# Strassen partial sums in a decoder trunk: banks emptied by ScalarE, the sum finished later on VectorE

## The chip, the core and the metric

The kernel is one program on one core of a Trainium2 chip. The metric is the device time of one execution in microseconds (us). A core has five engines that run side by side, each with a queue of its own: TensorE (PE in the profile, with its weight loads as PEld), VectorE (DVE), ScalarE (ACT), GpSimd (POOL) and SyncE (SP); the last two issue most of the DMA transfers here. A matmul adds its result into a bank of PSUM, the buffer that only TensorE, VectorE and ScalarE reach; a bank holds 128 x 512 float32.

## The reference

The reference is a trunk of two decoder layers on 512 tokens of width 1024. Each layer normalises, makes one wide projection, runs three attention-like branches, merges them by gates, projects and adds the residual. Then comes the part that the change touches, a squared-ReLU MLP:

```python
h = rmsnorm(x, norm_mlp_g[l])
x = x + jnp.square(jax.nn.relu(h @ w_up[l])) @ w_down[l]
```

with `w_up` of 1024 x 4096 and `w_down` of 4096 x 1024. A final RMSNorm closes the trunk. The result must agree with float32.

## The kernel before

Every operand of a product is split into a high and a low part of a matmul type that keeps fewer bits (`hi` by a cast on ScalarE, `lo` by a subtraction on VectorE, `split_to` and `Weights.split`), and each product is three matmuls: hi x hi, lo x hi, hi x lo. Weights come in by DMA, are split two units ahead (`W.pump`) into four pairs of buffers `whi`/`wlo`, and each unit is used by 12 or 24 matmuls.

The MLP runs over four groups `g` of 1024 hidden channels in each of the two layers. In groups 0 to 2 the down projection (512 x 1024 times 1024 x 1024) is done by Strassen's scheme in `strassen`: seven products of half-size blocks in place of eight. First eight calls of `tile_T` make the hidden activations, tile by tile (`put_h` squares them on ScalarE into the blocks `H[t, i, q]`, where tile m fills i = m // 4, q = m % 4 // 2). Sums and differences of these blocks are the left operands: `ready_early` after tile 3 makes those of P1 and P7, `ready_sums` after tile 7 makes S1 and S2 in two halves q (lines 1552 and 1553) and splits S2 for P6; P4, P5, P2 and P3 follow from `split_part` and `ready_s4`. The products run in the order P1, P7, P6, P4, P5, P2, P3, each as 24 matmuls (lines 1585 to 1587) in two units u of 12, into a pair of PSUM banks: P1, P6, P5 and P3 add up in the pair "B", P7 and P4 in "D", P2 in "A". A pair that goes on accumulating must be read out between two products: `add_to` (line 1598) reads both banks after P1 for the first output block, after P6 for the next, and so on. So it runs seven times a group, on two banks each time. An output block `acc[key]` that is not there yet is written by ScalarE (line 1605). One that is there is updated by one VectorE instruction that reads the bank, scales it and adds it (line 1607). In a layer's group 0 eight of the fourteen read-outs are first ones; groups 1 and 2 have none. After group 3's up projection has begun, `fold` transposes `acc` back and adds it to the residual.

The order is set in two steps. In the program, `defer(fn, delay)` puts evacuations and operand work in the queue `later`, which `run_later` serves as the dense products advance a clock of estimated nanoseconds; `need(name)` forces it. Then the compiler's scheduler lays the program out on the engines by a timeline of its own and may put instructions of one engine in another order than the program has them. On the chip each engine runs its own list in that fixed order, and semaphores hold an instruction back until its inputs and buffers are ready. Temporaries of 128 x 512 come from 42 slots (`get`, `put`).

Of the kernel before, what the change touches and what calls it, by code (L numbers as in the profile page):

```python
# [13 lines left out]
AF = mybir.ActivationFunctionType  # L14
ALU = mybir.AluOpType
# [33 lines left out]
class Weights:  # L49
# [33 lines left out]
    def block(self, kind, srcs):  # L83

        c = len(self.chunks)
        self.chunks.append((srcs, 4, 512))
        self.left.append(None)
        self.queues[kind].append(c)
        return c
# [138 lines left out]
def trunk_kernel(  # L228
# [15 lines left out]
    nc = tc.nc  # L244
# [12 lines left out]
    def get(dtype=F32):  # L257
        i = slots.popleft()
        t = sb.tile([P, 512], dtype, name=f"slot{i}", tag=f"slot{i}")
        owner[id(t)] = (i, t)  # L260
        return t

    def get2():
        return get(R), get(R)

    def put(*ts):
        for t in ts:
            slots.append(owner.pop(id(t))[0])
# [59 lines left out]
    clock = {"t": 0}  # L328
# [5 lines left out]
    def defer(fn, delay=0):  # L334
        later.append((clock["t"] + delay, fn))

    def run_later():
        while later and later[0][0] <= clock["t"]:
            later.popleft()[1]()

    def flush():
        while later:
            later.popleft()[1]()
# [53 lines left out]
    def drive(dense):  # L397
        for y in dense:
            if isinstance(y, tuple):
                if y[0] == "start":  # L400
                    live.append([y[1], clock["t"], y[2], None])
                elif y[0] == "finish":
                    finish()
                continue
            clock["t"] += y
            run_later()
            W.pump()
            advance()
# [172 lines left out]
    def split_to(hi, lo, src, g=None):  # L581

        if g is None:
            nc.scalar.copy(hi, src)
            nc.vector.tensor_sub(lo, src, hi.bitcast(F32))
        else:
            nc.scalar.activation(hi, src, AF.Copy, scale=g)
            nc.vector.scalar_tensor_tensor(lo, in0=src, scalar=g, in1=hi.bitcast(F32), op0=ALU.mult, op1=ALU.subtract)
# [42 lines left out]
    def tile_T(xs, evac):  # L631

        got, [(hi, lo)] = W.take()
        ps = dense_psum()
        nk = len(xs)
        yield from mm_T(ps, [hi[:, k] for k in range(nk)], [lo[:, k] for k in range(nk)], xs)
        W.done(got)
        evacuate(ps, lambda: evac(ps))
# [417 lines left out]
    def layer(l, box):  # L1056
# [381 lines left out]
        scale = {}  # L1438
# [14 lines left out]
        def put_up(m):  # L1453
            def go(ps):
                hi, lo = get2()
                h = get()
                nc.scalar.activation(h, ps, AF.Relu)
                nc.vector.tensor_mul(h, h, h)
                split_to(hi, lo, h)
                put(h)  # L1460
                hid[m] = (hi, lo)

            return go

        def put_down(m, final):
            def go(ps):
                t = get()
                nc.vector.tensor_mul(t, ps, rstd2_b)
                nc.vector.tensor_add(xm[m], xm[m], t)
                put(t)  # L1470
                if final:
                    new_x(m, G_MIX + (l + 1) * KD)
                    nc.gpsimd.dma_start(x_dram[l + 1][m], xm[m])
                    put(xm.pop(m))

            return go

        def put_last(m, c):
            def go(ps):
                q = get()  # L1480
                v = xm[m][:, c]
                nc.vector.tensor_mul(q[:, :256], ps[:, :256], rstd2_b[:, c])
                nc.vector.tensor_add(v, v, q[:, :256])
                nc.scalar.activation(q[:, :256], v, AF.Square)
                nc.scalar.activation(v, v, AF.Copy, scale=gain[:, G_FIN + m : G_FIN + m + 1])
                if m == KD - 1:
                    stats["t"] = q
                elif "s" not in stats:
                    stats["s"] = q
                else:  # L1490
                    nc.vector.tensor_add(stats["s"][:, :256], stats["s"][:, :256], q[:, :256])
                    put(q)

            return go

        def output(c):
            s, t = stats.pop("s"), stats.pop("t")
            r = to_rstd(token_sums([s, t], 2), D, 2)
            ps = rot(tt)
            spread_to(ps, r, 2)  # L1500
            for m in range(KD):
                nc.vector.tensor_mul(xm[m][:, c], xm[m][:, c], ps[:, :256])
                nc.sync.dma_start(out[m * P : (m + 1) * P, c], xm[m][:, c])
            put(s, t)


        acc = {}

        def strassen():

            H, parts = {}, {}
# [14 lines left out]

                return go

            def split_part(name, src, free=True):
                got = parts[name] = []  # L1530
                for q in range(2):
                    hi, lo = get2()
                    split_to(hi, lo, src[q])
                    got.append((hi, lo))
                if free:
                    put(*src)

            def block(t, i):
                return [H[t, i, q] for q in range(2)]
# [6 lines left out]
                    nc.vector.tensor_sub(s[q], H[0, 0, q], H[1, 0, q])  # L1546
                split_part("P7", s)

            def ready_sums():

                for q in range(2):
                    nc.vector.tensor_sub(H[1, 0, q], H[1, 1, q], H[1, 0, q])
                    nc.vector.scalar_tensor_tensor(
                        H[0, 0, q], in0=H[1, 0, q], scalar=-1.0, in1=H[0, 0, q], op0=ALU.mult, op1=ALU.subtract
                    )
                split_part("P6", block(0, 0), False)

            def ready_s4():

# [35 lines left out]
            def add_to(bank, i, j, sign):  # L1595


                def go():
                    for t in range(2):
                        ps = banks[bank][t]  # L1600
                        r = scale[sign][:, 2 * i + t : 2 * i + t + 1]
                        key = (2 * i + t, j)
                        if key not in acc:
                            acc[key] = get()
                            nc.scalar.activation(acc[key], ps, AF.Copy, scale=r)
                        else:
                            nc.vector.scalar_tensor_tensor(
                                acc[key], in0=ps, scalar=r, in1=acc[key], op0=ALU.mult, op1=ALU.add
                            )

                return go

# [6 lines left out]
            for m in range(KD):  # L1619
                yield from tile_T(X, put_h(m))  # L1620
                if m == 3:
                    defer(ready_early)
            defer(ready_sums)
            need("P1", parts)
            yield from product("P1", "B", True, False)
            defer(add_to("B", 0, 0, "+"))
# [23 lines left out]
            defer(give("B"))  # L1650

        def need(name, parts):
            while name not in parts:
                later.popleft()[1]()

        def fold(m):


            def go():
                ps = rot(tt)  # L1660
                for t in range(NT):
                    a = acc[t, m // 4][:, m % 4 * P : (m % 4 + 1) * P]
                    nc.tensor.transpose(ps[:, t * P : (t + 1) * P], a, ident)
                nc.vector.tensor_add(xm[m], xm[m], ps)
                if m % 4 == 3:
                    put(*(acc.pop((t, m // 4)) for t in range(NT)))

            return go

        for g in range(4):  # L1670
            if g < 3:
                if g == 2 and l < DEPTH - 1:
                    W.retired.extend(hold["pairs"])
                yield from strassen()
                continue
            for m in range(KD):
                defer(fold(m), 3000 + 4000 * m)
            if l < DEPTH - 1:
                W.retired.append(hold["wide"])
            for m in range(KD):  # L1680
                yield from tile_T(X, put_up(m))
            if (l, g) == (DEPTH - 1, 3):
                for hf in range(2):
                    c = slice(hf * 256, hf * 256 + 256)
                    for m in range(KD):
                        yield from tile_T(Later(hid, KD, c), put_last(m, c))
                    defer(lambda c=c: output(c))
                return
            for m in range(KD):
                yield from tile_T(Later(hid, KD), put_down(m, g == 3))  # L1690

            def free_h(hs):
                for hi, lo in hs:
                    put(hi, lo)

            hs = [hid.pop(k) for k in range(KD)]
            defer(lambda hs=hs: free_h(hs))
# [10 lines left out]
    def trunk():  # L1708
        for l in range(DEPTH):
            yield from layer(l, box)  # L1710
# [67 lines left out]
```

## Time and profile before

| | |
|---|---|
| median of 3 runs | 1824.52 us (1823.94 to 1825.95) |
| profiled execution | 1823.96 us, span 1822.2 us |
| PE busy | 1795.6 us (99%) |
| DVE busy | 1136.8 us (62%) |
| ACT busy | 805.5 us (44%) |
| POOL busy | 91.1 us (5%) |
| granted PE clock, mean | 0.997 |

The profiled execution's time is 1.76 us above its span; the span is what the profile resolves. PE is busy almost throughout, but its busy time counts overlapping matmuls, so how fast it goes is read from the spacing of matmul starts. Times in the rows below are microseconds from the start of the span.

### The profile page before, as it was taken

To read this page: it belongs to the slowest core of one execution; us is meant where nothing else is said; L and a number is where in the kernel's file an instruction comes from. 1 tells how busy PE (TensorE), PEld (TensorE's weight loads), DVE (VectorE), ACT (ScalarE), POOL (GpSimd) and SP (SyncE) were. 2 spreads that over 40 slices of the span, in tenths; PEclk is the share of its full clock that TensorE was granted. 3 is DMA by queue.
4 is the path that set the end of the run, shared out by engine and by line. 5 is a ranking of instruction groups with operands and counts; after the bars stand their busy time and mean duration, and the time that the engine had idled before them with its cause. 6 is when DMAs were issued, how large, how long until landed. Compare 5 with 4: busy or idle time off the path is not lost.

```text
span 1822.2 us, 22141 instructions
## 1 busy us (share of the span) xinstructions
PE 1795.6 (99%) x8848; PEld 1471.3 (81%) x8848; DVE 1136.8 (62%) x1746; ACT 805.5 (44%) x1359; POOL 91.1 (5%) x105
## 2 busy tenths in 40 slices
PE   8999999999999999999999999999999999999997
PEld 7878777788888887878898777778888888878787
DVE  6775755476464838575649657546755547475756
ACT  6644533143344644443346455422333346445344
POOL 1000000002000101000000000000020001010000
PEclk9999999999999999999999999999999999999999
DMA  6220222135632454512423112222274326362223
GB/s 188 85 90 25 83 82 70 58 93 152 183 99 87 119 158 103 175 47 93 133 79 104 47 37 83 82 81 69 70 204 142 93 93 170 107 171 84 93 95 114
DMA packets 150327, 188.59 MB, mean 103 GB/s; under 512 B 6608, under 2 KB 119776, under 8 KB 150224
## 3 DMA queue, kind: packets, MB, share of 16 engines
q1 hardware_dynamic: 137200, 154.42, 26.5%
q0 software_dynamic: 12352, 32.47, 7.0%
q8 instruction: 69, 1.13, 0.2%
q10 hardware_dynamic: 672, 0.29, 0.1%
q14 instruction: 34, 0.28, 0.0%
HBM read 182.97 MB, written 4.19 MB: 103 GB/s over the span
## 4 chain that ended last, share of the span: by engine, by line
PE 96%; DVE 3%; ACT 1%; issue 0%; DMA 0%; POOLq 0%; ACTq 0%; DVEq 0%
PE d L597 12%; PE d L599 12%; PE d L598 12%; PE z L597 8%; PE z L598 8%; PE z L599 8%; PE d L669 3%; PE d L671 3%; PE d L670 3%; PE z L1586 3%; PE t L717 3%; PE z L1587 3%; PE z L1585 3%; PE z L787 2%; PE t L709 2%; PE d L1585 1%
## 5 line engine op out<-in xcount | busy, mean ns | idle before, releaser
L179 ACT CAST whi<-raw 128x1024 fp32r<-128x1024 f32 (+1 forms) x206 | 214.9, 1046 | 394.1 <-PE d L598 138.1
L179 DVE TENSOR_TENSOR wlo<-raw,whi 128x1024 fp32r<-128x1024 f32 (+1 forms) x206 | 249.3, 1213 | 126.0 <-ACT whi L179 106.8
L597 PE MATMUL d<-xh,whi 128*128 128x512 f32 x656 | 261.9, 400 | 6.6 <-ACT whi L179 6.6
L599 PE MATMUL d<-xh,wlo 128*128 128x512 f32 x656 | 258.0, 393 | 0.0
L598 PE MATMUL d<-xl,whi 128*128 128x512 f32 x656 | 257.9, 393 | 0.0
L597 PE MATMUL z<-xh,whi 128*128 128x512 f32 x448 | 175.4, 392 | 0.0
L598 PE MATMUL z<-xl,whi 128*128 128x512 f32 x448 | 174.7, 390 | 0.0
L599 PE MATMUL z<-xh,wlo 128*128 128x512 f32 x448 | 173.4, 390 | 0.0
L597 PEld LDWEIGHTS d<-xh,whi 128*128 128x128 f32 x656 | 123.7, 188 | 33.4 <-ACT whi L179 6.6
L599 PEld LDWEIGHTS d<-xh,wlo 128*128 128x128 f32 x656 | 123.6, 188 | 26.3 <-DVE wlo L179 1.2
L598 PEld LDWEIGHTS d<-xl,whi 128*128 128x128 f32 x656 | 123.8, 189 | 24.3 <-issue 0.5
L597 PE MATMUL d<-slot,whi 128*128 128x512 f32 (+1 forms) x304 | 121.3, 399 | 0.0
L599 PE MATMUL d<-slot,wlo 128*128 128x512 f32 (+1 forms) x304 | 115.7, 381 | 0.0
L598 PE MATMUL d<-slot,whi 128*128 128x512 f32 (+1 forms) x304 | 115.5, 380 | 0.0
L669 PE MATMUL d<-whi,xh 128*128 128x512 f32 x256 | 102.4, 401 | 0.6 <-ACT slot L1109 0.5
L671 PE MATMUL d<-whi,xl 128*128 128x512 f32 x256 | 100.3, 393 | 0.0
L670 PE MATMUL d<-wlo,xh 128*128 128x512 f32 x256 | 100.1, 391 | 0.0
L599 PEld LDWEIGHTS z<-xh,wlo 128*128 128x128 f32 x448 | 84.1, 188 | 17.9 <-DVE wlo L179 0.4
L597 PEld LDWEIGHTS z<-xh,whi 128*128 128x128 f32 x448 | 84.1, 188 | 17.2
L598 PEld LDWEIGHTS z<-xl,whi 128*128 128x128 f32 x448 | 84.2, 188 | 17.1
L598 PE MATMUL z<-slot,whi 128*128 128x512 f32 (+1 forms) x272 | 95.2, 352 | 0.0
L597 PE MATMUL z<-slot,whi 128*128 128x512 f32 (+1 forms) x272 | 94.8, 352 | 0.0
(268 smaller groups left out, 3524.8 us busy)
## 6 DMA issues: line engine op xcount, KB each, us to landing
raw<-in_w_in_dram SPq DMA_DIRECT2D x53, 1024.0 KB, 5.1
raw<-in_w_down_dram SPq DMA_DIRECT2D x21, 1024.0 KB, 5.0
raw<-in_w_up_dram SPq DMA_DIRECT2D x20, 1024.0 KB, 6.0
work<-in_w_down_dram POOLq DMA_DIRECT2D x36, 512.0 KB, 6.6
aT<-in_w_up_dram SPq DMA_DIRECT2D x12, 1024.0 KB, 5.7
raw<-in_w_branch_dram SPq DMA_DIRECT2D x20, 512.0 KB, 3.5
aT<-in_w_down_dram SPq DMA_DIRECT2D x9, 1024.0 KB, 5.0
extra<-in_w_down_dram POOLq DMA_DIRECT2D x12, 512.0 KB, 9.1
```

What stands on the lines that cost most here:

```text
L179: self.last = (nc.scalar.copy(hi, src).ins, nc.vector.tensor_sub(lo, src, hi.bitcast(F32)).ins)
L597: nc.tensor.matmul(ps[:, :w], wh[k], h, start=(k == 0), stop=False)
L598: nc.tensor.matmul(ps[:, :w], wh[k], o, start=False, stop=False)
L599: nc.tensor.matmul(ps[:, :w], wl[k], h, start=False, stop=(k == n - 1))
L669: nc.tensor.matmul(ps[i], h, hi[:, kk], start=(k == 0), stop=False)
L670: nc.tensor.matmul(ps[i], h, lo[:, kk], start=False, stop=False)
L671: nc.tensor.matmul(ps[i], o, hi[:, kk], start=False, stop=(k == KD - 1))
L709: nc.tensor.transpose(ps[:, m * P : (m + 1) * P], a[:, e, j * P : (j + 1) * P], ident)
L717: nc.tensor.matmul(ps[e * 64 : (e + 1) * 64, j * P :], v[j][:, h * 64 : (h + 1) * 64], get_A(e, j), start=(j == 0), stop=(j == NT - 1), sk ...
L1585: nc.tensor.matmul(ps, h, hi[:, kk], start=begin and a, stop=False, skip_group_check=True)
L1586: nc.tensor.matmul(ps, h, lo[:, kk], start=False, stop=False, skip_group_check=True)
L1587: nc.tensor.matmul(ps, o, hi[:, kk], start=False, stop=end and z, skip_group_check=True)
```

## The change

`add_to` no longer updates an existing output block from the bank. ScalarE copies the scaled bank to a fresh slot, and a VectorE addition of that slot into `acc[key]` is put in a second queue, `slow`, with a delay of 11000 of the clock's nanoseconds; `slow` is emptied before the folds of group 3. Second, `ready_sums` is called for one half q at a time: for q = 0 after tile 5 and for q = 1 after tile 7, so the first half's S1, S2 and split come two tiles sooner in the program. `split_part` gets an argument for one half, and `need` waits for both halves.

```diff
+    slow = deque()
+
+    def postpone(fn, delay):
+
+        slow.append((clock["t"] + delay, fn))
+
     def run_later():
         while later and later[0][0] <= clock["t"]:
             later.popleft()[1]()
+        while slow and slow[0][0] <= clock["t"]:
+            slow.popleft()[1]()
@@
-            def split_part(name, src, free=True):
-                got = parts[name] = []
-                for q in range(2):
+            def split_part(name, src, free=True, only=None):
+                got = parts.setdefault(name, [])
+                for q in range(2) if only is None else (only,):
                     hi, lo = get2()
                     split_to(hi, lo, src[q])
                     got.append((hi, lo))
-                if free:
-                    put(*src)
+                    if free:
+                        put(src[q])
@@
-            def ready_sums():
-
-                for q in range(2):
-                    nc.vector.tensor_sub(H[1, 0, q], H[1, 1, q], H[1, 0, q])
-                    nc.vector.scalar_tensor_tensor(
-                        H[0, 0, q], in0=H[1, 0, q], scalar=-1.0, in1=H[0, 0, q], op0=ALU.mult, op1=ALU.subtract
-                    )
-                split_part("P6", block(0, 0), False)
+            def ready_sums(q):
+
+                nc.vector.tensor_sub(H[1, 0, q], H[1, 1, q], H[1, 0, q])
+                nc.vector.scalar_tensor_tensor(
+                    H[0, 0, q], in0=H[1, 0, q], scalar=-1.0, in1=H[0, 0, q], op0=ALU.mult, op1=ALU.subtract
+                )
+                split_part("P6", block(0, 0), False, q)
@@
                         else:
-                            nc.vector.scalar_tensor_tensor(
-                                acc[key], in0=ps, scalar=r, in1=acc[key], op0=ALU.mult, op1=ALU.add
-                            )
+                            a = get()
+                            nc.scalar.activation(a, ps, AF.Copy, scale=r)
+
+                            def add(a=a, key=key):
+                                nc.vector.tensor_add(acc[key], acc[key], a)
+                                put(a)
+
+                            postpone(add, 11000)
@@
                 yield from tile_T(X, put_h(m))
                 if m == 3:
                     defer(ready_early)
-            defer(ready_sums)
+                elif m in (5, 7):
+                    defer(lambda q=m % 4 // 2: ready_sums(q))
@@
         def need(name, parts):
-            while name not in parts:
+            while len(parts.get(name, ())) < 2:
                 later.popleft()[1]()
@@
                 yield from strassen()
                 continue
+            while slow:
+                slow.popleft()[1]()
             for m in range(KD):
                 defer(fold(m), 3000 + 4000 * m)
```

## Rows read from the trace of the kernel before

**Rows 1.** Page, part 1: busy time, share of the span, instructions.

```profile
PE 1795.6 (99%) x8848; PEld 1471.3 (81%) x8848; DVE 1136.8 (62%) x1746; ACT 805.5 (44%) x1359; POOL 91.1 (5%) x105
```

**Rows 2.** Waits of PE: who waited, for whom, us, times, longest.

```profile
PE d L1585 <- ACT slot L584: 3.3, 2, 1.7
...
PE d L1585 <- DVE slot L1607: 1.6, 2, 0.8
PE z L1585 <- DVE slot L1607: 1.5, 2, 0.7
```

**Rows 3.** Windows: length, busy of PE PEld DVE ACT POOL, PE clock, DMA.

```profile
610.00:620.00 10.00, 10.00 (x46) 8.27 (x45) 9.98 (x13) 8.63 (x14) 0.00 (x0) 1.00 0.02 5
700.00:710.00 10.00, 7.60 (x26) 5.59 (x25) 10.00 (x14) 3.98 (x6) 1.58 (x2) 0.84 0.15 52
1600.00:1610.00 10.00, 7.60 (x32) 5.31 (x31) 10.00 (x15) 4.00 (x6) 1.95 (x2) 1.00 0.15 53
```

**Rows 4.** Timeline of PE, layer 0, group 1, around its stall.

```profile
703.41 0.39 PE L1587 MATMUL d<-whi,slot 128*128 128x512 f32 x1
705.45 0.73 PE L1585 MATMUL d<-whi,slot 128*128 128x512 f32 x2 [1.65 <-ACT slot L584]
706.93 0.79 PE L1585 MATMUL z<-whi,slot 128*128 128x512 f32 x1 [0.75 <-DVE slot L1607]
...
711.32 0.63 PE L1586 MATMUL d<-wlo,slot 128*128 128x512 f32 x2
```

**Rows 5.** Timeline of PE, layer 1, group 1: ten spacings, then the stall's ends.

```profile
1600.72 0.39 PE L1586 MATMUL d<-wlo,slot 128*128 128x512 f32 x1
...
1602.98 0.39 PE L1587 MATMUL d<-whi,slot 128*128 128x512 f32 x1
...
1612.85 0.50 PE L1586 MATMUL z<-wlo,slot 128*128 128x512 f32 x1
```

**Rows 6.** Timeline of PE, group 2 of layer 0 and of layer 1.

```profile
789.84 0.39 PE L1587 MATMUL d<-whi,slot 128*128 128x512 f32 x1
...
791.85 0.50 PE L1585 MATMUL d<-whi,slot 128*128 128x512 f32 x1 [0.78 <-DVE slot L1607]
...
798.85 0.50 PE L1586 MATMUL z<-wlo,slot 128*128 128x512 f32 x1
...
1688.51 0.39 PE L1587 MATMUL d<-whi,slot 128*128 128x512 f32 x1
...
1697.52 0.50 PE L1586 MATMUL z<-wlo,slot 128*128 128x512 f32 x1
```

**Rows 7.** Timeline of DVE, layer 0, group 1.

```profile
697.67 1.40 DVE L1607 SCALAR_TENSOR_TENSOR slot<-d,rmlp,slot 128x512 f32<-128x512 f32 x2
...
703.13 0.68 DVE L1553 SCALAR_TENSOR_TENSOR slot<-slot,slot 128x512 f32<-128x512 f32 x1
```

**Rows 8.** Timeline of ACT, layer 0, group 1.

```profile
697.02 0.73 ACT L1524 ACTIVATE slot<-slot 128x256 f32<-128x256 f32 x2
...
703.83 1.04 ACT L167 CAST whi<-work 128x1024 fp32r<-128x1024 f32 x1 [1.38 <-PE d L1587]
704.78 0.61 ACT L584 CAST slot<-slot 128x512 fp32r<-128x512 f32 x1
```

**Rows 9.** Groups by line and form, whole span: count, busy us, mean ns.

```profile
L1607 DVE SCALAR_TENSOR_TENSOR slot<-z,rmlp,slot 128x512 f32<-128x512 f32 x24 | 16.9, 747 | 28.1 <-PE z L1587 28.1
L1552 DVE TENSOR_TENSOR slot<-slot,slot 128x512 f32<-128x512 f32 x12 | 8.3, 688 | 0.1
```

**Rows 10.** Timeline of ACT, layer 0: read-out in group 0, casts in group 2.

```profile
619.51 1.27 ACT L1605 ACTIVATE slot<-z,nmlp 128x512 f32<-128x512 f32 x2 [0.52 <-PE z L1587]
...
788.00 2.00 ACT L167 CAST whi<-work 128x1024 fp32r<-128x1024 f32 x2 [1.31 <-PE z L1587]
789.90 1.13 ACT L584 CAST slot<-slot 128x512 fp32r<-128x512 f32 x2
```

**Rows 11.** Timeline of DVE, layer 0, group 1: S1, first half.

```profile
688.26 0.69 DVE L1552 TENSOR_TENSOR slot<-slot,slot 128x512 f32<-128x512 f32 x1
```

## Prediction

> **What bounds the kernel now.** I read the page first, for the engines' shares. TensorE is busy 1795.6 of 1822.2 us, VectorE 62%, ScalarE 44% [rows 1]. So only TensorE's time counts, and a change on the other two engines can give back no more than what TensorE now loses to them. The waits of TensorE then say where that is: in the Strassen products it waits for line 584, the cast that makes the high part of a left operand, and for line 1607, the read-out of a bank by VectorE [rows 2]. The windows show when: in the crowded stretch behind a group's tiles VectorE is busy the whole 10 us while TensorE starts only 26 or 32 matmuls instead of 45 or 46 [rows 3]. The timelines of TensorE then give the size, which a list of waits gives too small, because a stall also slows the matmuls after it.
>
> Ten starts in a row take 2.26 us, so 0.226 us a matmul [rows 5]. For each stall I take the time between a matmul before it and one behind it, and subtract the matmuls that start in between, counted in the timeline, at 0.226. Layer 0, group 1: 7.91 us with 15 starts, 4.5 lost [rows 4]. Layer 1, group 1: 9.87 us with 27 starts, 3.8 lost [rows 5]. Group 2 of either layer: 9.01 us with 28 starts, 2.7 lost each time [rows 6]. Together **13.7 us**, and this is the ceiling of what the change can give. Group 0 has no such stall in either layer; its window has all 46 matmuls with VectorE at 9.98 of 10 us [rows 3].
>
> That is the best evidence in the profile. In group 0 the read-outs after P1, P7 and P6 already go by ScalarE, because those output blocks are new, and there one pair takes 1.27 us and starts 0.52 us after ScalarE fell idle, straight behind TensorE's last matmul [rows 10]. The change gives groups 1 and 2 the same three read-outs, and P4, P5, P2, P3 besides. The comparison is not clean, since in group 0 the tiles and products also run in another order on TensorE.
>
> **The change part by part.** *The read-out leaves VectorE.* 68 instructions of line 1607 go: 6, 14 and 14 in the three groups, twice. A pair of them holds VectorE for 1.32 us (1.40 with the end of the second) [rows 7]. In their place come 68 copies on ScalarE, 1.27 us a pair [rows 10], 43 us in all, and 68 additions of two slots on VectorE; the nearest row is the subtraction of two slots, 688 ns against 747 [rows 9], so VectorE saves 68 x 0.06 = 4 us overall. Neither sum counts by itself, as both engines have idle time; ScalarE goes from 44% to about 47%.
>
> What counts is the place. In layer 0, group 1 the queue of VectorE is: read-out of P1 at 697.67, then among other work line 1553 (S2, second half) at 703.13; the high part of that half is cast on ScalarE at 704.78, and TensorE, idle since 703.8, goes on at 705.45 [rows 4, 7, 8]. Without P1's read-out line 1553 moves up 1.32 us, to end about 702.4 instead of 703.7. ScalarE is then idle (it waits 1.38 us until 703.83 for the next weight cast [rows 8]), the cast of 0.61 us is done by 703.1, before TensorE needs it. The second wait there, 0.75 us for P7's read-out on VectorE [rows 4], also goes: P7 ends about 701 and ScalarE has the 1.27 us free before 705. What is late next is the weight cast at 703.83 and the low parts on VectorE; I leave 0.3 us for them. Layer 1 repeats the pattern. So in group 1 the change returns 4.5 + 3.8 - 0.6 = 7.7 us. 0.75 us of it is clock: the same stall came with a granted clock of 0.84 in layer 0 and 1.00 in layer 1 [rows 3], and I count it as returned with the stall.
>
> In group 2 the substitution is worth less. P7's last matmul starts at 789.84; TensorE waits at 791.85 for the first bank's read-out [rows 6]. ScalarE is then in two casts that end at 791.03 [rows 10], and two copies behind them end about 792.3, so the first bank would be free at about 791.7, hardly sooner than now. The second bank and the low parts behind the two read-outs do come sooner. Between nothing and 2.7 us I take half, 1.35 a layer, 2.7 in all.
>
> *The wait that is added.* A ScalarE copy now stands in ScalarE's queue until TensorE ends the product. Behind it stand the casts of left operands and of the next weights, and TensorE waits for these. The trace of before shows what such a place costs: the weight cast at 703.83 waited 1.38 us for TensorE, and the cast behind it, whose input was ready at 703.8, began only at 704.78 [rows 8]. The Trainium skill says the same of all such queues (PSUM — Partial Sum Buffer, section Engine vs sequencer instructions: ScalarE's and VectorE's queues are strictly first in, first out), and that rule speaks against the change: if the copies stand ahead of the critical cast, the sum would be that of the slower rival below instead of this one.
>
> *The postponed additions.* Two a product, 1.3 us, run about two products later in the program, or wherever the compiler finds VectorE idle. Behind the stall it is less full: 62% over the whole [rows 1]. Nobody waits for them but the next addition into the same block and, at the end, the fold. The last ones (P5, P2) are forced out before group 3, 3000 of the clock's nanoseconds ahead of the first fold; four of them take 2.6 us. I count nothing; if they come late, at most those 2.6 us a layer are lost.
>
> *The slots.* The copies take up to four slots more for about two products. From the code I count at most 36 of 42 in use at tile 7, when the last copies of the group before are long added, and fewer later. A wait for a slot is not in the trace; between 0 and one product of 24 x 0.226 = 5.4 us I take 0.
>
> *The first half two tiles sooner.* On the chip this is already so. Line 1552 for the first half runs at 688.26, while the squares of tile 7 come at 697.02 [rows 8, 11]: the compiler had pulled it ahead. It is worth 0; bounds are 0 and the 1.3 us of two such instructions a group if they were to leave the crowded stretch, 8 us over six groups, which the row excludes. No DMA is added or moved and no queue of SP or POOL is passed.
>
> **Sum.** 7.7 + 2.7 = 10.4 us. From the profiled execution's 1823.96 that gives 1813.6; its span is 1.76 us shorter, and the median of the runs is 0.56 above it. On the median's footing: 1824.52 - 10.4 = **1814**.
>
> **Rivals.** *No change.* The stall moves from VectorE's read-out to ScalarE's. The compiler lays all engines out anew, so TensorE's order in the products will differ, and waits of the present size can arise at other places. For it: in group 2 the copy is hardly sooner than the read-out it replaces, and VectorE stays full there with splits alone. Against it: group 0. Time 1822 to 1826, chance 0.19.
>
> *Slower: ScalarE becomes the bound behind the tiles.* Place: group 1, from tile 7's squares at 697.02 to the cast at 704.78. If P1's and P7's copies, 2 x 1.27 us, both stand ahead of that cast, they use up the 1.38 us of idle time and push the cast by 1.1 us; the same in four groups makes 4.6 us, and nothing is returned: 1829. It decides from the point where the cast ends later than 705.4. For it: ScalarE has no gap of note from 697 to 702. Against it: group 0, where 8.63 of 10 us on ScalarE did no harm [rows 3]. Chance 0.11.
>
> *Forecast.* Stalls mostly gone, 1810.5 to 1817, or a part of them, up to 1820.9: chance 0.70 together.
>
> **How the numbers follow.** Below stands the ceiling, 1824.5 - 13.7 = 1810.8, and a little more if waits that the intervals miss go too: 1809. Above, the forecast's case and the first part of the no-change case up to 1823.5 hold all but about 0.17. Faster or slower by 0.2% is 3.6 us, about what a measurement of this kernel can tell from no change. Faster 0.70, same 0.19, slower 0.11.
>
> **What would show it.** Right: in groups 1 and 2 the windows behind the tiles hold 45 or 46 matmuls, TensorE's waits name neither line 584 nor a read-out there, and the granted clock stays at 1.00 in layer 0, group 1; the read-outs are ScalarE rows that begin within half a microsecond of a product's end; the additions lie in VectorE's gaps; line 1552 keeps its place. Wrong: TensorE waits for the new copies, or for line 584 behind a copy that itself waits; new waits at weight casts or in group 0; waits of the folds for the last additions.

## The result and the profile after

The changed kernel takes **1837.11 us** (median of 5 runs, 1832.24 to 1840.81) against 1824.52: a ratio of 1.0065 with an interval of 1.0054 to 1.0077, so 12.6 us slower where 10.4 us faster was forecast. The profiled execution took 1838.09 us with a span of 1836.3, 14.1 us more than before. The runs of the changed kernel spread over 8.6 us, those of the kernel before over 2; what is split up below is the profiled execution. In the rows of after, line numbers behind the queue's code are higher by 7 to 13: the copies are line 1615, the additions line 1618, the products lines 1592 to 1594, the tiles lines 605 to 607, the splits of a block lines 592 and 593.

Page, part 1, of after; the answer to [rows 1]:

```profile
PE 1801.2 (98%) x8848; PEld 1478.0 (80%) x8848; DVE 1134.9 (62%) x1746; ACT 843.3 (46%) x1427; POOL 91.1 (5%) x105
```

The shares tell nothing: ScalarE has 68 instructions more, VectorE 2 us less. The waits of TensorE tell more (who waited, for whom, us, times, longest), beside [rows 2]:

```profile
PE z L605 <- ACT slot L1615: 9.9, 2, 5.6
...
PE z L1594 <- DVE slot L593: 3.5, 2, 1.7
...
PE z L1592 <- ACT whi L167: 1.9, 4, 0.7
...
PE z L1592 <- ACT slot L1615: 0.6, 2, 0.3
```

The three rows of before are gone. In their place the longest in these groups is a tile's first matmul into a bank that a ScalarE copy has yet to read, twice, once in each layer. The windows say where time is lost now (columns as in [rows 3]):

```profile
700.00:710.00 10.00, 9.47 (x41) 7.26 (x40) 10.00 (x15) 7.28 (x11) 1.95 (x2) 1.00 0.16 52
735.00:745.00 10.00, 5.69 (x15) 4.37 (x15) 5.83 (x6) 5.03 (x6) 0.00 (x0) 0.66 0.52 160
796.00:806.00 10.00, 7.52 (x20) 5.45 (x19) 9.61 (x13) 4.42 (x7) 0.00 (x0) 0.66 0.00 0
1606.00:1616.00 10.00, 9.47 (x41) 7.25 (x40) 10.00 (x15) 7.29 (x11) 1.95 (x2) 1.00 0.15 52
```

Behind group 1's tiles TensorE starts 41 matmuls in 10 us instead of 26 and 32: that part of the forecast came true. At the first tiles of group 2 (735 to 745) it starts only 15, and behind group 2's tiles (796 to 806) only 20. The kernel before, at group 2's first tiles and in its own stall behind them:

```profile
735.00:745.00 10.00, 10.00 (x45) 7.98 (x44) 5.01 (x6) 4.80 (x7) 0.00 (x0) 1.00 0.93 287
790.00:800.00 10.00, 8.74 (x34) 5.74 (x33) 10.00 (x13) 4.61 (x6) 0.00 (x0) 1.00 0.00 0
```

*The first tiles of group 2.* Timeline of TensorE in after, layer 0 and then layer 1:

```profile
734.79 0.39 PE L607 MATMUL z<-xh,wlo 128*128 128x512 f32 x1
739.49 0.79 PE L605 MATMUL z<-xh,whi 128*128 128x512 f32 x1 [4.31 <-ACT slot L1615]
740.08 0.63 PE L606 MATMUL z<-xl,whi 128*128 128x512 f32 x1
740.51 0.63 PE L607 MATMUL z<-xh,wlo 128*128 128x512 f32 x1
...
1640.64 0.39 PE L607 MATMUL z<-xh,wlo 128*128 128x512 f32 x1
1646.60 0.79 PE L605 MATMUL z<-xh,whi 128*128 128x512 f32 x1 [5.56 <-ACT slot L1615]
```

TensorE stands 4.5 and 5.7 us (the gap between starts less one spacing) and then goes on at the lower of its two clock levels, 0.43 us a matmul instead of 0.226. The whole loss, measured as the prediction measured stalls, is 7.0 us (734.79 to 744.69, 13 starts) and 8.6 us (1640.64 to 1652.64, 15 starts). ScalarE in the same stretch of after, and the DMA issue on SyncE's queue:

```profile
730.00 0.69 ACT L1615 ACTIVATE slot<-d,nmlp 128x512 f32<-128x512 f32 x1 [0.44 <-PE d L1594]
736.28 1.99 ACT L179 CAST whi<-raw 128x1024 fp32r<-128x1024 f32 x2 [5.59 <-DMA raw<-in_w_up_dram]
738.18 1.26 ACT L1615 ACTIVATE slot<-z,rmlp 128x512 f32<-128x512 f32 x2
739.33 1.04 ACT L179 CAST whi<-aT 128x1024 fp32r<-128x1024 f32 x1
```

```profile
722.46 3.01 SPq L110 DMA_DIRECT2D raw<-in_w_up_dram  x2
```

The copy at 738.18 is P2's, whose last matmul starts at 732.07. It could run at 732.5, but the compiler has put two weight casts ahead of it, and they wait 5.59 us for the transfer of `w_up` issued at 722 to 725. In the kernel before the same casts waited for the same transfer, which was issued later there, at 725.68, and TensorE lost only 0.25 us, at 739 (ScalarE, then VectorE):

```profile
732.65 1.05 ACT L179 CAST whi<-aT 128x1024 fp32r<-128x1024 f32 x1 [6.88 <-PE z L1587]
737.03 2.00 ACT L179 CAST whi<-raw 128x1024 fp32r<-128x1024 f32 x2 [3.33 <-DMA raw<-in_w_up_dram]
...
732.65 1.41 DVE L1607 SCALAR_TENSOR_TENSOR slot<-z,rmlp,slot 128x512 f32<-128x512 f32 x2 [5.21 <-PE z L1587]
```

There P2's bank was read by VectorE at 732.65, and the cast from `aT` stood ahead of the held ones. TensorE's order was another too: it ran product matmuls until 736.53 before it went on with the tiles, in after only until 732.07.

*The end of group 2.* VectorE in after, layer 0:

```profile
787.49 0.68 DVE L1618 TENSOR_TENSOR slot<-slot,slot 128x512 f32<-128x512 f32 x1
...
789.23 0.68 DVE L1618 TENSOR_TENSOR slot<-slot,slot 128x512 f32<-128x512 f32 x1
789.83 0.68 DVE L1559 TENSOR_TENSOR slot<-slot,slot 128x512 f32<-128x512 f32 x1
...
795.71 0.68 DVE L1618 TENSOR_TENSOR slot<-slot,slot 128x512 f32<-128x512 f32 x1
796.32 0.68 DVE L593 TENSOR_TENSOR slot<-slot,slot 128x512 fp32r<-128x512 f32 x1
796.92 0.68 DVE L1618 TENSOR_TENSOR slot<-slot,slot 128x512 f32<-128x512 f32 x1
...
799.26 0.68 DVE L593 TENSOR_TENSOR slot<-slot,slot 128x512 fp32r<-128x512 f32 x1
```

and TensorE:

```profile
797.74 0.50 PE L1592 MATMUL z<-whi,slot 128*128 128x512 f32 x1 [0.73 <-ACT whi L167]
799.99 0.79 PE L1594 MATMUL z<-whi,slot 128*128 128x512 f32 x1 [1.75 <-DVE slot L593]
```

Four additions, 0.6 us from start to start each, stand ahead of the low part at 799.26, and VectorE has no gap from the first of them to it: 2.4 us, more than the 1.75 us that TensorE waits for it. The 0.73 us at 797.74 is a wait for a weight cast on ScalarE; that the additions cause this one too isn't shown. The additions were to run later, and the compiler put them soon after their copies, between the operations that make S1, S2 and the low parts. Measured as in the prediction the stretch now loses 5.8 us in layer 0 (796.62 to 806.08, 16 starts) and 4.4 in layer 1 (1704.14 to 1710.61, 9 starts), where before it was 2.7 each.

**Where the 14.1 us come from.** Group 1's stall: 1.3 lost in each layer (703.56 to 710.97 and 1609.41 to 1616.82, 27 starts each), so a gain of 3.2 and 2.5; the 0.25 at 739 of before is gone too. First tiles of group 2: 7.0 and 8.6 lost. End of group 2: 3.0 and 1.65 more than before, by the table below. 15.6 + 4.65 - 5.95 = 14.3, against 14.1 between the spans; the rest is the rounding of the spacing. The starts of matmuls say the same for all kernels below. The table gives us from group 1's first product matmul to group 2's, and from there to the fourth fold of group 3, each for layer 0 / layer 1, worked out from the TensorE timelines (for the kernel before: 685.27 to 771.71, and to 835.12):

| kernel | G1 to G2 | G2 to fold |
|---|---|---|
| before | 86.44 / 85.52 | 63.41 / 63.44 |
| after | 89.90 / 91.55 | 66.45 / 65.09 |
| e4, P2 by VectorE | 88.52 / 89.90 | 62.37 / 62.37 |
| e1, casts behind P2's copy | 85.01 / 88.26 | 65.31 / 63.74 |
| e10, e1 with half of GpSimd's transfers | 84.07 / 84.03 | 63.67 / 65.06 |
| e7, three by ScalarE, additions behind | 83.79 / 83.79 | 63.17 / 63.17 |
| e8, additions behind splits | 82.38 / 82.38 | 62.03 / 62.03 |

### The profile page after: what moved, and what is told of

It is laid out like the page before. It is cut to its first block, busy times and chain, and to the rows that moved or that the text cites. A ratio compares the mean times of both kernels' runs of the same rounds, so it can differ in the third digit from the quotient of the medians.

```text
span 1836.3 us, 22220 instructions
## 1 busy us (share of the span) xinstructions
PE 1801.2 (98%) x8848; PEld 1478.0 (80%) x8848; DVE 1134.9 (62%) x1746; ACT 843.3 (46%) x1427; POOL 91.1 (5%) x105
## 4 chain that ended last, share of the span: by engine, by line
PE 94%; DVE 2%; DMA 2%; ACT 1%; issue 0%; POOLq 0%; ACTq 0%; DVEq 0%
PE d L605 12%; PE d L607 12%; PE d L606 12%; PE z L605 8%; PE z L606 8%; PE z L607 8%; PE d L677 3%; PE d L679 3%; PE d L678 3%; PE z L1594 3%; PE z L1592 3%; PE z L1593 3%; PE t L725 3%; PE t L717 2%; PE z L795 2%; DMA raw<-in_w_up_dram 1%
```

## The experiments

All were timed beside the kernel before; ratios are to it. The theory on trial: the change does what it says at group 1, and the loss is a matter of order, a copy behind casts that wait for a transfer and additions ahead of splits. The rivals: the halves of part two; ScalarE's extra work as such; a transfer that is late whatever the order.

**e2, part two alone.** The kernel before with `ready_sums(q)` after tiles 5 and 7, read-outs as before.

> Only the second part of the change: S1 and S2 by halves, the first half after tile 5; all later read-outs by VectorE from the bank as before. If that part does nothing, because the compiler had pulled the first half ahead already: 1824.5, within 1 us, and the same four stalls as before (13.7 us). If it carries part of the loss: above 1826. If it helps by itself: below 1822.

Measured: 1825.17 us, ratio 1.000 (0.9991 to 1.0009). The waits are those of [rows 2]. Part two does nothing, neither good nor bad.

**e4, P2's banks read by VectorE as before**, the other six by ScalarE:

```diff
+                        elif bank == "A":
+                            nc.vector.scalar_tensor_tensor(
+                                acc[key], in0=ps, scalar=r, in1=acc[key], op0=ALU.mult, op1=ALU.add
+                            )
```

> The changed kernel, but P2's two banks are read out by VectorE into the output block as before (4 of 68 read-outs in each layer are moved back at most). Theory A: no ScalarE copy of P2 is left to stand behind a cast that waits for DMA, so this too comes to about 1821 (1818 to 1825). Theory B: 1835 to 1840. The new order of the lists may move other waits by some us, as theory A says nothing of them.

Measured: 1832.62 us, ratio 1.0046 (1.0029 to 1.0063). First the longest wait of TensorE in these groups, then ScalarE and TensorE there:

```profile
PE z L605 <- ACT whi L179: 8.8, 2, 5.2
```

```profile
736.67 1.99 ACT L179 CAST whi<-raw 128x1024 fp32r<-128x1024 f32 x2 [5.11 <-DMA raw<-in_w_up_dram]
738.57 1.04 ACT L179 CAST whi<-aT 128x1024 fp32r<-128x1024 f32 x1
...
739.66 0.50 PE L605 MATMUL z<-xh,whi 128*128 128x512 f32 x1 [3.61 <-ACT whi L179]
```

P2's copy is gone and the stall stays. TensorE goes on at 739.66, as the cast from `aT` ends: that one too stood behind the two that wait for the transfer. So the copy was one victim of the order and the cast from `aT` another; what holds the queue is the pair of casts ahead of both. The end of group 2, on the other hand, is mended in this run with no edge at all: group 2 to the fold takes 62.37 us in the table, TensorE's wait for a low part is gone, and VectorE's list has a single addition (796.10) between S1 at 787.33 and the low part at 796.70. That agrees with the additions' place as the cause there, with the copies of the six other products left on ScalarE.

**e1, the weight casts behind P2's copy.** An ordering edge on ScalarE from P2's copy to the weight casts that follow it in the program:

```diff
-                            nc.scalar.activation(a, ps, AF.Copy, scale=r)
+                            i_read = nc.scalar.activation(a, ps, AF.Copy, scale=r).ins
+                            if bank == "A":
+                                W.read = i_read
@@ in the weight casts
+            if self.read is not None:
+                self.behind(self.last[0], self.read)
```

> The changed kernel, but the weight casts of the tiles keep behind the ScalarE copy of P2's banks that precedes them in the program (an order on one engine, no work added or removed). Theory A: the loss is that this copy stands behind two casts that wait for a DMA of w_up, and TensorE waits for the banks (4.3 and 5.6 us, 7.1 and 8.9 with the slow clock after them); then both waits go and the time is 1837 - 16 = 1821 (1818 to 1824), with less spread. Theory B: the DMA is simply late and TensorE would have waited for the weights instead; then the wait changes its name to the weight cast and the time stays at 1835 to 1840. Theory C, the additions crowd VectorE: this run leaves that as it is, so the loss in group 2 (5.7 and 4.4 us) stays.

Measured: 1831.7 us, ratio 1.0035 (1.0024 to 1.0047); half, as the expectation had it for neither theory. Waits of TensorE, then ScalarE:

```profile
PE z L610 <- ACT whi L180: 4.6, 2, 3.4
PE z L1599 <- DVE slot L598: 3.5, 2, 1.8
```

```profile
732.41 1.27 ACT L1620 ACTIVATE slot<-z,rmlp 128x512 f32<-128x512 f32 x2 [1.80 <-PE z L1599]
733.57 1.05 ACT L180 CAST whi<-aT 128x1024 fp32r<-128x1024 f32 x1
735.68 2.94 ACT L180 CAST whi<-raw 128x1024 fp32r<-128x1024 f32 x3 [1.07 <-DMA raw<-in_w_up_dram]
```

P2's copy and the cast from `aT` now run when their inputs are there, and the stall shrinks from 9.9 to 4.6 us of waiting. What is left is the transfer itself, which TensorE, back at the tiles at 732.21, asks for before it has landed: the casts from `raw` wait 1.07 us in layer 0 and 3.24 in layer 1. The end of group 2 still has its wait for a low part.

**e5, e1 and the additions behind the splits; e8, the additions alone.** In e8 the weight casts are left to the compiler:

```diff
-            nc.vector.tensor_sub(lo, src, hi.bitcast(F32))
+            last_lo["i"] = nc.vector.tensor_sub(lo, src, hi.bitcast(F32)).ins
@@
-                                nc.vector.tensor_add(acc[key], acc[key], a)
+                                i = nc.vector.tensor_add(acc[key], acc[key], a).ins
+                                tc.add_manual_dep(i, last_lo["i"].name, order, reason="behind the splits")
```

> As the first of these runs, and besides each postponed addition keeps behind the last split of a left operand that precedes it in the program, on VectorE. Theory C (the compiler pulls the postponed additions back into the crowded stretch, where they take the place of the read-outs): the stalls of group 2 shrink from 5.7 and 4.4 us to 1 each, so 8 us less than the first run, about 1813 (1810 to 1816). Rival: the stalls of group 2 come from the order of the splits themselves; then within 2 us of the first run.

> The change, with one thing added: a postponed addition on VectorE keeps the place behind the low part of the last split that the program issues ahead of it; the weight casts are left where the compiler puts them. Theory A (the additions, taken forward into the crowded stretch, cost group 2, and the layout that the compiler makes around them costs the first tiles of the next group as well): 1815, as the run that orders both, and no wait of TensorE for line 179 or for a copy's slot at group 2's first tiles. Rival B (the order of the weight casts behind P2's copy was needed for the first tiles): group 2's end is mended (-6), the first tiles keep their stall: 1829 to 1831.

Measured: e5 1814.82 us, ratio 0.9946 (0.9932 to 0.9961); e8 **1814.2 us, ratio 0.9944 (0.993 to 0.9959)**, faster than both kernels. The same edge is worth 22.9 us on the changed kernel and 16.9 on e1. TensorE's waits in e8 that lie in the Strassen groups:

```profile
PE z L1594 <- ACT slot L1617: 1.9, 2, 0.9
...
PE z L1594 <- ACT whi L167: 0.7, 2, 0.3
```

VectorE behind group 2's tiles, and ScalarE ahead of group 2's first tiles, in e8:

```profile
781.21 0.68 DVE L1561 TENSOR_TENSOR slot<-slot,slot 128x512 f32<-128x512 f32 x1
781.82 1.29 DVE L595 TENSOR_TENSOR slot<-slot,slot 128x512 fp32r<-128x512 f32 x2
783.02 0.68 DVE L1562 SCALAR_TENSOR_TENSOR slot<-slot,slot 128x512 f32<-128x512 f32 x1
...
787.10 1.28 DVE L1620 TENSOR_TENSOR slot<-slot,slot 128x512 f32<-128x512 f32 x2
```

```profile
730.36 1.27 ACT L1617 ACTIVATE slot<-z,rmlp 128x512 f32<-128x512 f32 x2 [7.26 <-PE z L1596]
731.51 1.05 ACT L179 CAST whi<-aT 128x1024 fp32r<-128x1024 f32 x1
732.45 1.06 ACT L179 CAST whi<-raw 128x1024 fp32r<-128x1024 f32 x1
733.40 1.27 ACT L1617 ACTIVATE slot<-d,nmlp 128x512 f32<-128x512 f32 x2
734.57 1.99 ACT L179 CAST whi<-raw 128x1024 fp32r<-128x1024 f32 x2
```

S1 and S2 come first and the additions after them; and no cast waits for the transfer in layer 0 (one waits 0.33 us in layer 1), though it is issued at 722.56 and lands after a median of 8.5 us, in after at 722.46 and after 8.8. One edge on VectorE mends the first tiles too, so the edge of e1 was not needed: the order on ScalarE and on TensorE comes out otherwise. TensorE's order is visible: in after the last 22 product matmuls end and the tiles go on at 732.30, in e8 the last 35 stand together and the tiles go on at 733.78, as 35 stood together in the kernel before, with the tiles at 736.76. How the compiler's scheduler gets from the one to the other is in no trace, and stays open.

**e11, no additions.** The copies are made and dropped, so only the first product of each output block reaches the output.

> The change with the postponed additions left out (the partial sums are copied by ScalarE and dropped, so only the first product of each block is in the output). Theory A (the additions are what costs): group 2's end is at most 1 us above its work and the time is about 1815, the ordered version's. Rival B (the copies on ScalarE cost, wherever the additions stand): the stall of some 4 us at the end of the groups and that at the first tiles stay, 1829 to 1837.

Measured: 1812.68 us, ratio 0.9935 (0.9919 to 0.9952). So ScalarE's 68 copies are no net loss. Additions behind the splits cost 1.5 us (1814.2 against 1812.7), where the compiler puts them by itself 24.4 (1837.1). The comparison has two flaws: VectorE has 68 operations less than in e8, and the first transposes of the folds stand among the products, since they have no addition to wait for.

**e10, half of GpSimd's transfers left out**, on top of e1 (the combined blocks of weights lack a term):

```diff
-        for n, src in enumerate(srcs):
+        for n, src in enumerate(srcs[:1]):
```

> The kernel with the weight casts ordered behind P2's copy (1831.7), less the second half of the transfers that GpSimd's queue adds up for the combined blocks of weights: only the first source of each sum is loaded, so the sums lack a term. Theory A (the w_up transfers of group 2's first tiles come late because they share the DMA engines with those of GpSimd): they land about 5 us after their issue instead of up to 11, the wait of 1.2 and 3.4 us for the weight cast at those tiles goes, 1825 to 1828. Rival B (they are late because they are issued late, once their buffers come free): landing and wait stay, 1830 to 1833.

Measured: 1821.84 us, ratio 0.9987 (0.9978 to 0.9997), more than theory A asked for. ScalarE in e10, and then the DMA row of the stretch 715 to 745 (issues, KB each, median us to landing), where e1 has 8.7:

```profile
733.98 1.05 ACT L180 CAST whi<-aT 128x1024 fp32r<-128x1024 f32 x1
734.91 2.95 ACT L180 CAST whi<-raw 128x1024 fp32r<-128x1024 f32 x3
```

```profile
raw<-in_w_up_dram SPq DMA_DIRECT2D x2, 1024.0 KB, 6.6
```

The issue time is nearly that of e1 (722.76 against 722.39), the landing is 2.1 us sooner, the casts from `raw` no longer wait, and TensorE's wait for them is gone in both layers but for 0.5 us each for a low part. So the late part was contention with the accumulating transfers on GpSimd's queue. Group 1 to group 2 shrinks by 0.94 and 4.23 us, most of the 5.9 us between the profiled executions. The medians differ by 9.9; how much of the rest is the spread of the runs (e1's lie between 1828.1 and 1833.0) and how much other stretches, where transfers were left out too, isn't shown.

**e7, only P1, P7 and P6 by ScalarE**, their additions behind the splits, the other four from the bank by VectorE:

```diff
+                        elif (bank, i, j) in (("D", 1, 0), ("B", 1, 1), ("A", 0, 0), ("B", 0, 1)):
+                            nc.vector.scalar_tensor_tensor(
+                                acc[key], in0=ps, scalar=r, in1=acc[key], op0=ALU.mult, op1=ALU.add
+                            )
```

> Only the banks of P1, P7 and P6 are read out by ScalarE with a postponed addition that stays behind the splits; P4, P5, P2 and P3, where VectorE is less full, are read and added by VectorE from the bank as before. Theory A (what the change can give comes from the crowded stretch behind the tiles alone): 1815, the same as with all seven by ScalarE. Rival B (ScalarE's copies of the later four give a part too, or keep the layout that has no stall at the first tiles): 1818 to 1830.

Measured: 1819.09 us, ratio 0.997 (0.9959 to 0.9981). The crowded stretch alone does not explain the gain: with all seven it is 4.9 us larger. In the table 1.4 us of it lie between group 1 and group 2 and 1.1 behind group 2, in each layer. Waits that are longer here than in e8:

```profile
PE z L1594 <- ACT slot L1621: 2.5, 2, 1.2
...
PE z L1594 <- ACT whi L167: 1.4, 2, 0.7
```

Both lie behind group 2's tiles, where TensorE's and ScalarE's orders differ from e8's again; so this run does not separate the worth of the four later copies from that of the order.

## Why the prediction failed, step by step

**Group 1, 7.7 us: right in the mechanism, too high by a quarter.** Its stalls fell from 4.5 and 3.8 us to 1.3 each, where 0.3 had been left for the rest, the clock in layer 0 came back from 0.84 to 1.00, and the gain is 5.7 us (7.2 in e8, over the whole stretch from group 1 to group 2). The read-outs went to ScalarE, and line 1553's successor starts at 702.57 instead of 703.13.

**Group 2, 2.7 us: right in size, but not in this kernel, and by luck.** With the additions behind the splits e8 gains 1.38 and 1.41, 2.8 in all. As compiled, after loses 3.0 and 1.65. The 1.35 a layer was half of a stall that nothing in the rows split in two.

**"The postponed additions. I count nothing": the step that failed.** The text let them run "about two products later in the program, or wherever the compiler finds VectorE idle" and looked at the average of 62% behind the stall. They ran soon after their copies, in the one stretch with no idle VectorE. The 11000 of the clock's nanoseconds order the program, not the engine's list. The expected bound, 2.6 us a layer before the folds, sat at the wrong place. The rival without change named what came, waits of the present size "at other places", and gave it no price of its own. e8 shows the price of this step with all that follows from it: 22.9 us (1837.1 less 1814.2). e11, without additions, runs 1812.7: the rest of the change is no net loss.

**"The wait that is added": the right queue, the wrong place.** The prediction priced a ScalarE copy standing ahead of casts behind the tiles. What occurred is the mirror image, at the end of the group: a copy and a cast stand behind casts that wait for a transfer, 7.0 and 8.6 us. The strict order of a queue that the text quoted from the Trainium skill (PSUM — Partial Sum Buffer, section Engine vs sequencer instructions) is borne out by e4 and e1: the cast from `aT` started at 738.57 behind held casts and at 733.57 ahead of them. The row that could have told was there: ScalarE's wait of 3.33 us for `w_up` at 737.03 in the kernel before, harmless while VectorE read P2's bank and TensorE had products to run until 736.53. About half of the waiting was this order (9.9 us to 4.6 in e1); the other half was the transfer, slowed by GpSimd's, that TensorE reached before it had landed (e10).

**Halves and slots, 0: right.** e2 gives 1.000, and in after the copies wait for TensorE alone, never for a slot. (In e8 a cast of a left operand waits 0.6 us for an addition, once in each layer; that may be a slot.)

**The rival on the other side.** "ScalarE becomes the bound behind the tiles", 1829 at 0.11, had the engine and the sign; the place was another, and the price, 15.6 us, over three times the 4.6 it was given. The forecast of 1814 is what e8 runs, 7.2 + 2.8 = 10.0 us against 10.4, which owes part to the guess for group 2.

## What to carry to other kernels

Work that is moved off the critical place must be given a new place on its engine's list; a delay in program order does not hold where a scheduler reorders, so order it behind the work that it must not displace and look where it landed. Before an engine takes over a read-out that another engine waits for, look for every instruction on that engine that already waits for a DMA: a wait that is harmless now holds back whatever is put behind it. And price a transfer's landing against the time at which the faster kernel will ask for it.

## What the runs showed of the hardware

A stall costs more than its length. The 4.5 us at the first tiles of layer 0 became 7.0 and the 5.7 us of layer 1 became 8.6: the matmuls behind them ran at 0.43 us a start, the 1.2 GHz level, until the clock rose. The same two waits at the end of group 2 (0.73 and 1.75 us in both layers) came with a granted clock of 0.66 over 10 us in layer 0 and 0.83 in layer 1, and that end cost 5.8 and 4.4 us.

GpSimd's transfers slow those of SyncE: with half of GpSimd's loads of `w_down` left out, the 1 MB loads of `w_up` on SyncE's queue landed after a median of 6.6 us instead of 8.7 (layer 1: 6.4 instead of 10.0).
